# In-projection of a hybrid decoder trunk: the norm's scale moved from the products to the operand, convolution taps from PSUM

## The chip, the cores and the metric

The kernel runs on one core of one Trainium2 chip. The metric is the device time of one execution in microseconds; the kernel before takes 3083.93 us (median of three runs, 3083.13 to 3099.12).

## What is computed

A decoder of two layers on 1040 tokens (16 learned tokens and 1024 of the sequence) with 1024 channels:

```python
for layer in range(DEPTH):                                  # 2
    hn = rmsnorm(h, norm_mix_w[layer])                      # h * rsqrt(mean(h*h) + eps) * w
    proj = hn @ w_in[layer]                                 # 1024 x 3336
    hq, hf, hi, hg, gq, gk, gv, gz, ga, gb, su = split(proj)
    y_a = hgrn2_mixer(hq, hf, hi, hg, ...)
    y_b = gdn_mixer(gq, gk, gv, gz, ga, gb, conv_w, ...)    # qkv = silu(causal_conv4(concat(gq, gk, gv)))
    y_c = s5_mixer(su, ...)
    h = h + concat(y_a, y_b, y_c) @ w_out[layer]
    h = h + square(relu(rmsnorm(h, norm_mlp_w[layer]) @ mlp_w1[layer])) @ mlp_w2[layer]
return rmsnorm(h, final_norm_w)[:, N_META:]
```

The convolution is causal, per channel, with four taps: token t needs the products of t-3 to t.

## The kernel before

Channels lie on the partitions and tokens along the free axis, so `h` is eight tiles of 128 channels (`KD`). The tokens are worked in two blocks of 520 (`T`); a block (l, b) is layer l, tokens b. The dense products are made in halves: an operand x is split into a high part (`xh`) and the rest (`xl`), weights likewise (`wh`, `wl`), and a product of 128 columns is, for each of eight k, the three pairs xh wh, xl wh, xh wl on two runs of 260 tokens (`HN`): 48 matmuls into one PSUM tile `pd` of two banks. Two `pd` tiles exist. A weight granule of four k is loaded by DMA, its high part made by ScalarE (`wh`, L458) and its low part by GpSimd, POOL in the profile (`wl`).

Before a block, `normed` makes xh and xl of h times the norm's weight, tile by tile, as the tiles of h are finished; the norm's scale, one number per token, is not in them. `square` adds up the squares of h, `scale` turns their sum (a matmul with ones on all partitions) into the tile `r` with Ln and Exp. Each product is then multiplied by `r` when VectorE takes it out of PSUM (`scaled`). The two S5 products come first and are taken out before `r` is known (`late`), and are multiplied by it afterwards.

`block` then runs the in-projection and the mixers: two S5 products, the eight gate columns (`in_rows`: decay and beta of the gated DeltaNet, worked on 4 to 8 partitions, stored as `rowd`), twelve convolution products (`in_conv`), four z gates, and for each pair of HGRN2 heads q, f, i and a gate. `in_conv` writes the scaled product into a scratch tile `raw` behind three tokens that the block before left in `hist`, keeps its own last three there, makes the first tap on ScalarE and the other three on VectorE from SBUF:

```python
nc.vector.tensor_copy(raw[:, 0:3], self.hist[:, i, :])
self.scaled(raw[:, 3:T + 3], ps)
nc.vector.tensor_copy(self.hist[:, i, :], raw[:, T:T + 3])
self.act(cv, raw[:, 3:T + 3], AF.Copy, scale=w(3))
for t in range(3):
    self.stt(cv, raw[:, t:t + T], w(t), cv, ALU.mult, ALU.add)
```

A clamp, the sigmoid (three ScalarE passes), a multiplication on POOL and a store follow. Scratch tiles of 520 tokens have the tag `s`; there are six. In the names of the trace `s<-pd,r` is a scaling out of PSUM, `s<-s,cvw` a tap, `mh`, `nh` and `mt` are scratch of the mixers, `mx` their PSUM.

A scheduler sets the order on each engine: it takes the traced instructions with their priorities (weights are called 1000 instructions ahead) and a model of their times, and writes one fixed order per engine. The engines run it in order and wait on semaphores. Layer 0's blocks are both projected at the start; while the state recurrences of block (0, 0) run, block (0, 1) is projected. Layer 1's blocks each follow an output projection and MLP: those of (0, 0), then block (1, 0), those of (0, 1), then block (1, 1). The mixers of a block run beside the next dense work.

## Time and profile before

| | before |
|---|---|
| median of three runs | 3083.93 us |
| lowest, highest | 3083.13, 3099.12 us |
| span of the profiled execution | 3076.0 us |
| TensorE matmul busy | 92% of the span |
| VectorE, ScalarE, POOL busy | 55%, 42%, 52% |
| mean granted TensorE clock | 0.958 |

The profiled execution's own time is not listed apart from the runs; its span lies 7.9 us under their median, the part of a run outside the first and the last instruction. The clock is the share of full speed that was granted to TensorE. It has two levels, 1.2 and 2.4 GHz, so 0.9 over a stretch means the lower level in a fifth of it. Matmuls of one engine overlap; their busy time in a stretch of pure dense work is all of it.

### The profile page before, as it was taken

How to read it: one execution, taken by the hardware profiler on the slowest of the kernel's cores; microseconds unless marked ns; L12 is line 12 of the kernel's file. 1: busy time of each engine (PE TensorE's matmuls, PEld its weight loads, DVE VectorE, ACT ScalarE, POOL GpSimd, SP SyncE). 2: the span in 40 equal slices, each digit the busy share in tenths (PEclk: the TensorE clock that was granted, in tenths of full speed). 3: DMA queues.
4: the chain of work that ended last, by engine and by line, in shares of the span. 5: the costliest groups of instructions: out<-in, count | busy, mean ns of one | idle time of the engine just before them, and what ended most of it. 6: DMA issues, size and time to landing. Idle time of an engine off the chain costs nothing.

```text
span 3076.0 us, 60588 instructions
## 1 busy us (share of the span) xinstructions
PE 2841.1 (92%) x23513; PEld 2652.0 (86%) x23513; DVE 1703.3 (55%) x3079; ACT 1292.1 (42%) x2621; POOL 1598.3 (52%) x1377
## 2 busy tenths in 40 slices
PE   7777899879999998888999999888999999999998
PEld 7677789879999997878989999887777788999998
DVE  7899976686532248897553224887544322522224
ACT  5534465434443344434443334444544333433332
POOL 3564757465644446746364444677464444444442
PEclk8898899889999999899999999889999999999999
DMA  5646455644433354555443335455443333533332
GB/s 150 189 116 189 138 142 160 167 92 136 126 91 102 93 152 125 153 134 147 131 121 99 91 92 152 124 152 135 136 120 106 98 93 97 160 93 92 91 93 80
DMA packets 641613, 381.20 MB, mean 124 GB/s; under 512 B 166239, under 2 KB 599237, under 8 KB 641325
## 3 DMA queue, kind: packets, MB, share of 16 engines
q1 hardware_dynamic: 641325, 377.31, 44.0%
q8 instruction: 186, 3.05, 0.4%
q14 instruction: 102, 0.84, 0.1%
HBM read 308.52 MB, written 70.43 MB: 123 GB/s over the span
## 4 chain that ended last, share of the span: by engine, by line
PE 58%; DVE 13%; DMA 4%; issue 3%; ACT 2%; POOL 1%; SPq 0%; DVEq 0%; POOLq 0%; ACTq 0%
PE pd L124 49%; PE mxt L124 6%; DVE mh L112 4%; DVE s L115 2%; PE mxh L124 2%; DVE s L112 1%; ACT s L109 1%; DVE s L120 1%; DVE nh L112 1%; DMA wr<-in_w_in_dram 1%; DMA nh<-rowd 1%; DVE xl L115 0%; DMA D<-D 0%; DMA hdr<-h 0%; DVE h L112 0%
## 5 line engine op out<-in xcount | busy, mean ns | idle before, releaser
L112 POOL TENSOR_TENSOR wl<-wr,wh 128x512 fp32r<-128x512 f32 x776 | 1056.1, 1363 | 1128.1 <-ACT wh L458 1021.2
L124 PE MATMUL pd<-xh,wh 128*128 128x260 f32 (+2 forms) x3688 | 833.0, 300 | 50.3 <-DVE s L112 31.5
L124 PE MATMUL pd<-xl,wh 128*128 128x260 f32 (+2 forms) x3688 | 833.1, 299 | 10.9 <-DVE xl L115 8.6
L124 PE MATMUL pd<-xh,wl 128*128 128x260 f32 (+1 forms) x3624 | 817.1, 300 | 18.8 <-POOL wl L112 18.3
L458 ACT CAST wh<-wr 128x512 fp32r<-128x512 f32 x776 | 476.8, 617 | 834.3 <-PE pd L124 731.4
L124 PEld LDWEIGHTS pd<-xh,wh 128*128 128x128 f32 (+1 forms) x3688 | 596.0, 194 | 71.5 <-issue 33.7
L124 PEld LDWEIGHTS pd<-xh,wl 128*128 128x128 f32 x3624 | 588.9, 194 | 37.1 <-POOL wl L112 22.7
L124 PEld LDWEIGHTS pd<-xl,wh 128*128 128x128 f32 (+1 forms) x3688 | 596.6, 193 | 27.5 <-DVE xl L115 9.6
L124 PE MATMUL pd<-uh,wh 128*128 128x260 f32 (+1 forms) x2008 | 470.4, 303 | 10.3 <-DVE h L112 4.6
L124 PE MATMUL pd<-ul,wh 128*128 128x260 f32 (+1 forms) x2008 | 470.8, 302 | 0.0
L124 PE MATMUL pd<-uh,wl 128*128 128x260 f32 (+1 forms) x2008 | 469.2, 302 | 0.3 <-POOL wl L112 0.3
L112 DVE TENSOR_TENSOR h<-h,pd 128x520 f32<-128x520 f32 (+2 forms) x296 | 200.1, 677 | 389.0 <-PE pd L124 386.5
L109 ACT ACTIVATE s<-s 128x520 f32<-128x520 f32 (+3 forms) x431 | 272.2, 635 | 256.5 <-DVE s L120 169.1
L124 PEld LDWEIGHTS pd<-uh,wh 128*128 128x128 f32 x2008 | 322.5, 190 | 25.9 <-issue 5.4
L124 PEld LDWEIGHTS pd<-uh,wl 128*128 128x128 f32 x2008 | 322.7, 189 | 13.8 <-POOL wl L112 0.7
L124 PEld LDWEIGHTS pd<-ul,wh 128*128 128x128 f32 x2008 | 322.9, 190 | 12.9 <-issue 0.2
L115 DVE SCALAR_TENSOR_TENSOR s<-pd,r 128x520 f32<-128x520 f32 (+2 forms) x137 | 94.1, 691 | 327.4 <-PE pd L124 327.1
L112 DVE TENSOR_TENSOR ul<-s,uh 128x520 fp32r<-128x520 f32 (+1 forms) x129 | 96.2, 747 | 142.3 <-ACT uh L458 142.2
L115 DVE SCALAR_TENSOR_TENSOR s<-s,cvw 128x520 f32<-128x520 f32 x144 | 152.2, 1060 | 16.3 <-ACT s L109 15.4
L112 POOL TENSOR_TENSOR s<-s 128x520 f32<-128x520 f32 x80 | 114.5, 1431 | 51.5 <-ACT s L109 45.0
L112 POOL TENSOR_TENSOR mh<-mh,qh 128x260 f32<-128x260 f32 (+5 forms) x128 | 98.6, 794 | 25.5 <-ACT mh L109 22.1
L112 DVE TENSOR_TENSOR s<-s 128x520 f32<-128x520 f32 (+3 forms) x119 | 98.8, 835 | 15.5 <-ACT s L109 13.6
(250 smaller groups left out, 3302.0 us busy)
## 6 DMA issues: line engine op xcount, KB each, us to landing
wr<-in_mlp_w_dram SPq DMA_DIRECT2D x512, 256.0 KB
wr<-in_w_in_dram SPq DMA_DIRECT2D x208, 256.0 KB
wr<-in_w_out_dram SPq DMA_DIRECT2D x64, 256.0 KB
qkvd<-s SPq DMA_DIRECT2D x48, 260.0 KB
win<-qkvd SPq DMA_DIRECT2D x40, 312.0 KB
hdr<-h SPq DMA_DIRECT2D x32, 260.0 KB
mh<-qkvd SPq DMA_DIRECT2D x40, 208.0 KB
hd<-s SPq DMA_DIRECT2D x32, 260.0 KB
```

Of the source, the lines that this page charges most:

```text
L109: return self.nc.scalar.activation(out, in_, func, **kw)
L112: return (eng or self.nc.vector).tensor_tensor(out, a, b, op)
L115: return self.nc.vector.scalar_tensor_tensor(out, a, s, b, op0, op1)
L120: return e.tensor_scalar(out, a, s1, None, op0)
L124: return self.nc.tensor.matmul(out, lhsT, rhs, start=start, stop=stop, **kw)
L458: self.nc.scalar.copy(hi, src)
```

## The change

In the in-projection alone, `normed_rows` takes the place of `normed`: all eight squares first, then `scale`, then for each tile of h one VectorE pass that multiplies by weight and scale into an `s` tile, and the split of that. The operand is four tokens longer (`HIST`): in front of the block's tokens stand the last four normed tokens of the block before (zeros in the first), put there and kept by POOL. `in_conv` asks for 264 instead of 260 tokens of each run, so that every run contains the products of the tokens before it, and takes all four taps straight from PSUM. Nothing multiplies by the scale after a product any more: the gates clamp out of PSUM, HGRN2's f takes its negative part on VectorE and its positive part on ScalarE, its i is copied by ScalarE, the S5 products are turned to chunks on the way out of PSUM, one half by each of the two engines. `gdn_begin` copies the three groups of gate rows that are needed instead of all. The MLP's norm and products are as before.

```diff
+    def normed_rows(self, h, wcol, b):
+        nc = self.nc
+        xs = [], []
+        acc = self.s()
+        for k in range(KD):
+            self.square(acc, h[k], k)
+        self.squares, self.r = acc, None
+        r = self.scale()
+        if b == 0:
+            self.hist = self.tl(self.big, [128, KD, HIST], "hist", 1)
+        for k in range(KD):
+            w = self.prm[:, wcol + k:wcol + k + 1]
+            xn = self.tl(self.sp, [128, T + 8], "s", N_S)[:, :T + HIST]
+            if b == 0:
+                nc.gpsimd.memset(xn[:, :HIST], 0.0)
+            else:
+                nc.gpsimd.tensor_copy(xn[:, :HIST], self.hist[:, k])
+            self.stt(xn[:, HIST:], h[k], w, r, ALU.mult, ALU.mult)
+            if b == 0:
+                nc.gpsimd.tensor_copy(self.hist[:, k], xn[:, T:])
+            hi, lo = self.operand("xh"), self.operand("xl")
+            nc.scalar.copy(hi, xn)
+            self.tt(lo, xn, hi.bitcast(F32), ALU.subtract)
+            xs[0].append(hi)
+            xs[1].append(lo)
+        return xs
...
     def in_conv(self, l, b, xs, i):
-        ps = self.cols(l, C_GQ + 128 * i, xs)
-        raw = self.tl(self.sp, [128, T + 8], "s", N_S)
-        nc.vector.tensor_copy(raw[:, 0:3], self.hist[:, i, :])
-        self.scaled(raw[:, 3:T + 3], ps)
-        nc.vector.tensor_copy(self.hist[:, i, :], raw[:, T:T + 3])
-        cv = self.s()
+        ps = self.cols(l, C_GQ + 128 * i, xs, {c: slice(c * HN, (c + 1) * HN + HIST) for c in range(2)})
+        cv, sg = self.s(), self.s()
         w = lambda t: self.cvw[:, l * 48 + t * 12 + i:l * 48 + t * 12 + i + 1]
-        self.act(cv, raw[:, 3:T + 3], AF.Copy, scale=w(3))
+        at = lambda t: ps[:, :, HIST - 3 + t:HIST - 3 + t + HN]
+        self.act(self.half(cv), at(3), AF.Copy, scale=w(3))
         for t in range(3):
-            self.stt(cv, raw[:, t:t + T], w(t), cv, ALU.mult, ALU.add)
+            self.stt(self.half(cv), at(t), w(t), self.half(cv), ALU.mult, ALU.add)
         self.ts(cv, cv, NEG, ALU.max)
...
+    def in_silu(self, l, xs, col):
+        t, n = self.s(), self.s()
+        self.ts(self.half(n), self.cols(l, col, xs)[:, :, :HN], NEG, ALU.max)
+        self.silu(n, t)
+        return t
...
     def in_s5(self, l, xs):
-        products = [lambda t=t: self.cols(l, C_SU + 128 * t, xs) for t in range(2)]
-        return [self.spill(u, "ud", 4) for u in self.late(products, True)]
+        n = (NC + 1) // 2 * CH
+        us = []
+        for t in range(2):
+            ps = self.cols(l, C_SU + 128 * t, xs, {0: slice(HIST, HIST + n), 1: slice(HIST + n, HIST + T)})
+            u = self.s()
+            for c, copy in ((0, self.nc.vector.tensor_copy), (1, self.nc.scalar.copy)):
...
     def in_hgrn(self, l, xs, j):
-        r = self.half(self.scale())
-        self.stt(self.half(mn), ps, 0.0, r, ALU.min, ALU.mult)
-        self.stt(self.half(mx), ps, 0.0, r, ALU.max, ALU.mult)
+        self.ts(self.half(mn), ps, 0.0, ALU.min)
+        self.act(self.half(mx), ps, AF.Relu)
...
-        self.scaled(vt, ps)
+        self.nc.scalar.copy(self.half(vt), self.cols(l, C_HI + 128 * j, xs)[:, :, :HN])
...
     def block(self, l, b, h, hook=None, first=False):
-        xs = self.normed(h, 8 * l)
+        xs = self.normed_rows(h, 8 * l, b)
```

The scheduler writes a new order for the whole program. Three places of it follow; in them `xN` behind a row means that it stands N times in a row, and line numbers of the change are one higher.

VectorE, the norm of block (1, 0), behind the MLP of block (0, 0). Before (`h<-h,pd` adds a product of the MLP to h, `s<-s` adds a square, `ul<-ys,uh` belongs to the next output projection):

```order
L112 TENSOR_TENSOR h<-h,pd 128x520
L112 TENSOR_TENSOR ul<-ys,uh 128x520
L115 SCALAR_TENSOR_TENSOR xl<-h,prm,xh 128x520
L112 TENSOR_TENSOR s<-s 128x520
L112 TENSOR_TENSOR h<-h,pd 128x520
L112 TENSOR_TENSOR ul<-ys,uh 128x520 x2
L115 SCALAR_TENSOR_TENSOR xl<-h,prm,xh 128x520
L112 TENSOR_TENSOR s<-s 128x520
L112 TENSOR_TENSOR ul<-ys,uh 128x520
L538 COPY s<-pd 128x520 x2
L112 TENSOR_TENSOR s<-s,r 128x65x8 x2
```

The change, from the last addition to h:

```order
L113 TENSOR_TENSOR h<-h,pd 128x520
L113 TENSOR_TENSOR ul<-ys,uh 128x520
L113 TENSOR_TENSOR s<-s 128x520
L113 TENSOR_TENSOR ul<-ys,uh 128x520
L116 SCALAR_TENSOR_TENSOR s<-h,prm,r 128x520 x6
L113 TENSOR_TENSOR xl<-s,xh 128x524 x5
L116 SCALAR_TENSOR_TENSOR s<-h,prm,r 128x520
L113 TENSOR_TENSOR xl<-s,xh 128x524
L116 SCALAR_TENSOR_TENSOR s<-h,prm,r 128x520
L113 TENSOR_TENSOR xl<-s,xh 128x524 x2
L676 COPY s<-pd 128x33x8 x2
```

Before, seven of the eight operand tiles stand between the additions to h, and one behind the last; now sixteen operations stand between the last addition and the first eviction.

TensorE at the same place. Before, the sum of squares (`pd<-s,ones`) stands behind the S5 products:

```order
L124 MATMUL pd<-xh,wh 128x260 x2
L124 MATMUL pd<-xl,wh 128x260 x2
L124 MATMUL pd<-xh,wl 128x260 x2
L124 MATMUL pd<-s,ones 128x260 x2
L124 MATMUL pd<-xh,wh 40x260
```

The change (`uh,wl` ends the MLP's last product):

```order
L125 MATMUL pd<-uh,wl 128x260 x2
L125 MATMUL pd<-s,ones 128x260 x2
L125 MATMUL pd<-xh,wh 128x264
L125 MATMUL pd<-xh,wh 128x256
L125 MATMUL pd<-xh,wh 128x264
L125 MATMUL pd<-xh,wh 128x256
L125 MATMUL pd<-xl,wh 128x264
```

Between the MLP's last product and the first S5 product nothing else stands on TensorE.

POOL at the same place in the change (before, the row of `wl` simply goes on):

```order
L113 TENSOR_TENSOR wl<-wr,wh 128x512 x76
L518 MEMSET s 128x4 x6
L523 COPY hist<-s 128x4 x6
L518 MEMSET s 128x4 x2
L523 COPY hist<-s 128x4 x2
L113 TENSOR_TENSOR wl<-wr,wh 128x512
```

The sixteen pieces of four tokens stand in one row, and the next granule's low part behind them.

## Rows read from the trace of the kernel before

**Rows 1.** The page's part 1: busy time of each engine, share of the span, instructions.

```profile
PE 2841.1 (92%) x23513; PEld 2652.0 (86%) x23513; DVE 1703.3 (55%) x3079; ACT 1292.1 (42%) x2621; POOL 1598.3 (52%) x1377
```

**Rows 2.** Busy time by stretch; columns: stretch, its length, engines, PEclk, DMA share, GB/s.

```profile
20.00:282.00 262.00, 204.09 (x1467) 193.90 (x1466) 230.82 (x486) 121.14 (x245) 136.35 (x100) 0.87 0.55 148
282.00:400.00 118.00, 96.22 (x1059) 88.83 (x1059) 104.50 (x188) 56.17 (x123) 76.85 (x70) 0.90 0.60 169
400.00:590.00 190.00, 177.69 (x1677) 162.72 (x1675) 119.94 (x232) 100.58 (x239) 112.92 (x110) 0.94 0.53 148
1165.00:1363.00 198.00, 160.84 (x1221) 156.55 (x1219) 182.29 (x342) 88.46 (x182) 124.45 (x92) 0.91 0.53 137
1937.00:2129.00 192.00, 153.20 (x1166) 148.40 (x1165) 164.44 (x244) 88.31 (x183) 133.58 (x102) 0.89 0.54 142
1700.00:1800.00 100.00, 100.00 (x837) 100.00 (x836) 24.55 (x36) 32.83 (x53) 44.83 (x35) 1.00 0.31 91
```

**Rows 3.** The chain of waits, by line, in the stretch 1165 to 1363.

```profile
by line: DVE s L115 18.8%; DVE mh L112 16.8%; issue 11.1%; DVE s L112 6.7%; DVE s L120 6.0%; ACT s L109 5.7%; DVE nh L112 5.3%; DVE RT L112 3.2%; DVE s L620 2.6%; DVE s L629 2.2%; DMA diag<-MAd 2.2%; DVE xl L112 2.0%; DMA rowd<-s 1.9%; DVE 
```

**Rows 4.** Timeline of VectorE: first and last of twelve convolution evictions (start, length, what).

```profile
1165.11 0.70 DVE L112 TENSOR_TENSOR s<-pd,r 128x520 f32<-128x520 f32 x1
...
1261.73 0.69 DVE L112 TENSOR_TENSOR s<-pd,r 128x520 f32<-128x520 f32 x1
```

**Rows 5.** Groups by line and shape, VectorE: count, busy us, mean ns, idle before.

```profile
L115 DVE SCALAR_TENSOR_TENSOR s<-s,cvw 128x520 f32<-128x520 f32 x144 | 152.2, 1060 | 16.3 <-ACT s L109 15.4
L115 DVE SCALAR_TENSOR_TENSOR s<-pd,r 128x520 f32<-128x520 f32 x105 | 72.6, 696 | 251.6 <-PE pd L124 251.3
L120 DVE TENSOR_SCALAR s<-s 128x520 f32<-128x520 f32 x84 | 66.5, 792 | 1.0
L112 DVE TENSOR_TENSOR s<-pd,r 128x520 f32<-128x520 f32 x88 | 60.7, 689 | 27.8 <-PE pd L124 25.5 <-DMA hd<-s 2.1
L115 DVE SCALAR_TENSOR_TENSOR xl<-h,prm,xh 128x520 fp32r<-128x520 f32 x56 | 51.8, 932 | 15.9 <-ACT xh L109 15.9
L631 DVE COPY hist<-s 128x3 f32<-128x3 f32 x48 | 24.0, 499 | 0.8
L629 DVE COPY s<-hist 128x3 f32<-128x3 f32 x48 | 21.7, 453 | 2.4 <-POOL s L112 1.5 <-DMA qkvd<-s 0.8
L112 DVE TENSOR_TENSOR s<-s,r 128x520 f32<-128x520 f32 x14 | 19.6, 1459 | 21.6 <-ACT r L109 21.6
```

**Rows 6.** The tile of the taps' weights: min/median/max ns; idle before, and until what.

```profile
L115 DVE SCALAR_TENSOR_TENSOR s<-s,cvw x144: 721/758/4155, 67.1 to 2034.2; 128x520 f32<-128x520 f32 x144
  DMA rowd<-s: 21.4, 4
```

**Rows 7.** Timeline, the norm of block (1, 0): last addition to h up to the scale.

```profile
1140.33 0.68 DVE L112 TENSOR_TENSOR h<-h,pd 128x520 f32<-128x520 f32 x1
...
1141.68 0.62 ACT L109 ACTIVATE s<-h 128x520 f32<-128x520 f32 x1
...
1143.93 0.69 DVE L112 TENSOR_TENSOR s<-s 128x520 f32<-128x520 f32 x1
1147.99 0.69 DVE L538 COPY s<-pd 128x520 f32<-128x520 f32 x1
...
1151.78 1.04 PE L124 MATMUL pd<-s,ones 128*128 128x260 f32 x4
...
1154.36 0.60 ACT L109 ACTIVATE r<-pd 128x520 f32<-128x520 f32 x1
1154.98 0.64 ACT L109 ACTIVATE r<-r 128x520 f32<-128x520 f32 x1
```

**Rows 8.** Groups, POOL: the weights' low parts, and the smallest copy.

```profile
L112 POOL TENSOR_TENSOR wl<-wr,wh 128x512 fp32r<-128x512 f32 x776 | 1056.1, 1363 | 1128.1 <-ACT wh L458 1021.2 <-PE pd L124 27.2 <-DMA mh<-in_s_lam_im_dram 18.4
...
L1186 POOL COPY SC<-CB 8x80 f32<-8x80 f32 x8 | 3.2, 396 | 4.2 <-DVE CB L1179 3.8
```

**Rows 9.** Busy time and granted clock just after TensorE had waited.

```profile
1190.00:1192.00 2.00, 2.00 (x12) 2.00 (x11) 2.00 (x3) 2.00 (x5) 1.79 (x2) 0.50 0.80 250
```

More of the change, by code (lines that the diff above doesn't have):

```diff
@@ L44 @@
 TINY = 1e-19
+HIST = 4
 GELU_C = 2.0 * math.sqrt(2.0 / math.pi)
@@ L469, in granule_now @@
         if keep:
-            lo, hi = [self.tl(self.big, [128, T], tag, 8, F32R)[:, :512].rearrange("p (k m) -> p k m", k=4) for tag in ("xl", "xh")]
+            lo, hi = [self.operand(tag)[:, :512].rearrange("p (k m) -> p k m", k=4) for tag in ("xl", "xh")]
         else:
@@ L482, in product, with columns @@
     def product(self, wts, xs, runs=None):
+        ps = self.columns(wts, xs, {c: self.run_of(c) for c in runs or self.runs})
+        return ps[:, :len(self.runs), :self.nh]
+    def columns(self, wts, xs, runs):
         xh, xl = xs
@@ L488, in product, with operand @@
             for i, (w, x) in enumerate(((wh, xh), (wh, xl), (wl, xh))):
-                for c in runs or self.runs:
-                    self.mm(ps[:, c, :self.nh], w[:, k % 4, :], x[k][:, self.run_of(c)],
+                for c, cs in runs.items():
+                    self.mm(ps[:, c, :cs.stop - cs.start], w[:, k % 4, :], x[k][:, cs],
                             start=(k == 0 and i == 0), stop=(k == kn - 1 and i == 2))
-        return ps[:, :len(self.runs), :self.nh]
+        return ps
+    def operand(self, tag):
+        return self.tl(self.big, [128, T + HIST], tag, 8, F32R)
+    def normed_rows(self, h, wcol, b):
[24 more added lines that the diff above has]
+        return xs
     def normed(self, h, wcol):
@@ L499, in normed @@
             w = self.prm[:, wcol + k:wcol + k + 1]
[L500 to L501 removed]
+            hi, lo = self.operand("xh")[:, :self.nt], self.operand("xl")[:, :self.nt]
             self.act(hi, h[k], AF.Copy, scale=w)
@@ L526, in scale, with late @@
         return self.r
-    def scaled(self, out, ps):
-        self.tt(self.half(out), ps, self.half(self.scale()[:out.shape[0]]), ALU.mult)
-    def late(self, products, chunks):
+    def late(self, products):
         ts = []
@@ L536, in late, with cols @@
             t = self.s()
-            if chunks:
-                self.nc.vector.tensor_copy(self.half(t), product())
-            else:
-                self.act(self.half(t), product(), AF.Relu)
+            self.act(self.half(t), product(), AF.Relu)
             ts.append(t)
-        if not chunks:
-            for t in ts:
-                self.tt(t, t, self.scale(), ALU.mult)
-            return ts
-        os = [self.s() for _ in ts]
-        for o, t in zip(os, ts):
-            c = lambda a: a.rearrange("p (c j) -> p c j", j=CH)
-            self.tt(o.rearrange("p (j c) -> p c j", j=CH), c(t), c(self.scale()), ALU.mult)
-        return os
+        for t in ts:
+            self.tt(t, t, self.scale(), ALU.mult)
+        return ts
     def silu(self, n, out):
-        self.ts(n, n, NEG, ALU.max)
         self.sigma(out, n)
         self.tt(out, out, n, ALU.mult, eng=self.nc.gpsimd)
-    def cols(self, l, col, xs):
-        return self.product(self.ready.pop((l, col), None) or self.in_weights(l, col), xs)
+    def cols(self, l, col, xs, runs=None):
+        wts = self.ready.pop((l, col), None) or self.in_weights(l, col)
+        return self.columns(wts, xs, runs or {c: slice(HIST + c * HN, HIST + (c + 1) * HN) for c in range(2)})
     def in_weights(self, l, col):
@@ L591, in in_rows @@
         self.tt(xv, xv, ps[32:40, :, :HN], ALU.add)
-        self.tt(x[0:8], x[0:8], self.scale()[0:8], ALU.mult)
         self.ts(u[0:8], x[0:8], NEG, ALU.max)
@@ L1261, in out_mlp @@
             nc.sync.dma_start(t, self.YS[b][k][:, T - self.nt:])
-            for half_, (tag, bufs) in zip(xs, (("uh", NY), ("ul", NY)) if k < NY else (("xh", 8), ("xl", 8))):
-                half_.append(self.tl(self.big, [128, T], tag, bufs, F32R)[:, :self.nt])
+            for half_, tag in zip(xs, ("uh", "ul") if k < NY else ("xh", "xl")):
+                half_.append((self.tl(self.big, [128, T], tag, NY, F32R) if k < NY else self.operand(tag))[:, :self.nt])
             self.split(t, xs[0][k], xs[1][k])
@@ L1316, in halves @@
             return step
-        for t in self.late([lambda j=j: hidden(0, j) for j in range(2)], False):
+        for t in self.late([lambda j=j: hidden(0, j) for j in range(2)]):
             second_operand(0, t)
```

43 lines of the change are left out of this document (17 added, 26 removed).

## Prediction

> **What bounds the kernel now.** I read the page's busy times first, then the same by stretch, then the chain of waits in one stretch, and the groups last. Over the whole span TensorE is busy 92% and VectorE 55% [rows 1], which looks like a TensorE kernel; that is an average over two kinds of stretch. In the MLPs (1700 to 1800) TensorE is busy all the time at full clock, 837 matmuls in 100 us or 0.12 us each, so a product of 48 takes 5.7 us, and VectorE is busy a quarter [rows 2]. In the in-projections it is the other way round: VectorE is busy 88% from 20 to 282 (block (0, 0)), 89% from 282 to 400 (first part of (0, 1)), 92% from 1165 to 1363 (block (1, 0)) and 86% from 1937 to 2129 (block (1, 1)), while TensorE waits and its granted clock falls to 0.87 to 0.91 [rows 2]. Only the second part of (0, 1), 400 to 590, belongs to TensorE (94%). In (1, 0) twelve convolution products are evicted between 1165.11 and 1261.73 [rows 4], 8.8 us apart, where TensorE would need 5.7. The chain of waits there names VectorE: its nine lines that the row shows sum to 64%, the taps (line L115) first with 18.8% [rows 3].
>
> So VectorE time taken out of these four stretches can become time, and work on any engine elsewhere can't.
>
> **What it relieves.** All prices are means of groups, for one block of 520 tokens.
> - A convolution loses the scaling out of PSUM (0.689) and two copies of three columns (0.499 and 0.453), and its three taps change their source [rows 5]. A tap from SBUF takes 1.060 on average though the median is 0.758 and the worst 4.155 [rows 5, 6]; the same operation with one operand in PSUM takes 0.696 [rows 5]. The new tap isn't in the trace; I bound it by 0.69 and 1.06 and take 0.696, its nearest row in operation, shape and source. 0.689 + 0.952 + 3 x 0.364 = 2.73 us, twelve times 32.8.
> - Eight gates (six, and q twice) lose a pass: 0.689 + 0.792 becomes one clamp out of PSUM at 0.69 [rows 5]. 8 x 0.79 = 6.3.
> - HGRN2's f: two passes of 0.696 become one [rows 5], the other goes to ScalarE; twice, 1.4. Its i goes to ScalarE whole: 2 x 0.689 = 1.4.
> - S5: a copy of 0.69 [rows 7] and a turning multiplication of 1.459 [rows 5] become half a turned copy. Between half of the one and half of the other, 0.35 and 0.73, I take 0.5: 2 x 1.65 = 3.3.
>
> Together 45.2 us a block. ScalarE gets the moved reads (one out of PSUM took 0.60 [rows 7]); it is busy 45% in these stretches [rows 2], so I price them at nothing; without that cover they would be about 4 us a block. POOL gets 8 to 16 pieces of four columns, at most 0.40 each [rows 8], and is busy 63% of (1, 0) [rows 2]; nothing as well, unless something waits for them (below). TensorE gets four columns more in 2304 matmuls: at 0.12 us for 260 columns 1.8 ns each, 4 us in all.
>
> **What it adds: the norm.** The operand took one VectorE pass of 0.932 a tile and now takes two [rows 5]: 8 x 0.93 = 7.5 us more (5.5 at the 0.69 of an unhindered pass [rows 7]). In layer 0 this comes off the relief, 45.2 - 7.5 = 37.7. In layer 1 the old pass lay under the MLP, and the new ones stand in front of the projection, where TensorE waits.
>
> That wait is the price of the change. In (1, 0) the last addition to h begins at 1140.33 and the first S5 product is evicted at 1147.99, 7.7 us later, without a gap on TensorE. Now the path is addition 0.68, square 0.62, sum 0.69, matmuls with ones 1.04, Ln 0.60, Exp 0.64 [rows 7], some 4.8 us with six hand-offs of under 0.1; then sixteen VectorE passes at 0.69 to 0.93, 11.0 to 14.9 us, since the order puts all of them in front of the first eviction; then the last tile's matmuls, 0.7. That is 16.5 to 20.4 instead of 7.7. The matmuls with ones no longer stand behind the S5 products, which gives 1.0 back: 8 to 12 us. The order has nothing for TensorE to do in between. After such a pause the clock is at the lower level for a while, 0.50 from 1190 to 1192 [rows 9]; 10 us with that. In (0, 0) VectorE's part is counted already, so only the path to the scale is left: 5 us. In (0, 1) the scale can be made beside the recurrences of (0, 0): 2 us.
>
> **The sum.** How much of the relief becomes time I take from the two rows on (1, 0): 0.64 by the chain, 0.92 by the busy share; 0.8. TensorE leaves room for it: a mean clock of 0.91 over 198 us costs 18 of its 161 busy us, so it needs 143, and VectorE would need 182 - 42 = 140.
> - (0, 0): 0.8 x 37.7 - 5 = -25.
> - (0, 1): half of the relief, 22.6 - 7.5 = 15.1, lies in the first part, x 0.8 = 12; of the other half, where TensorE is the bound, I take a quarter, 6; less 2: -16.
> - (1, 0) and (1, 1): the relief without S5, which lies ahead of the stretch, 41.9 x 0.8 - 10 = -23.5 each.
>
> With 4 us of columns that is -84 us. Against the profiled span of 3076.0 it makes 2992; the median of the runs, 3083.93, lies 7.9 above that span, so **3000 us**. With 0.64, no quarter and the dearer waits (13, 13, 8, 3) it is 3038, with 0.92, half of the rest of (0, 1) and the cheaper ones (8, 8, 3, 0) 2966.
>
> **One rule against it.** The taps of one product now read PSUM three times, and the trace says that this is cheaper, 0.696 against 1.060 [rows 5]. The Trainium skill, page "VectorE: DVE Perf Modes", section "Rules for kernel authors", says otherwise: either accept the basic rate from PSUM, or copy to SBUF first if many operations follow. By that rule the taps bring nothing; it is the fourth rival below.
>
> **The rivals.**
> 1. *The projection is paced by scratch, not by VectorE: no change.* Six `s` tiles serve everything; ScalarE sat idle 21.4 us in front of four first taps until the store of the gate rows had freed one [rows 6]. A convolution now holds its PSUM tile until scratch is there and all four taps are done, with two such tiles. If only 0.3 of the relief arrives (41 of 136.6) and the waits cost 27 and the columns 4, it is 3074. Against it: VectorE at 92%. 0.13.
> 2. *The norm becomes a barrier: slower.* POOL's pieces stand between VectorE's passes (scratch, zeros, multiplication, copy), and the low parts of the next weights behind them. With 16 pieces of 0.40 in the path (6.4), three low parts of 1.36 behind it [rows 8] (4.1), all passes at 0.93 (14.9), one product at half clock (5.7 more) and the 5.5 of path and last tile, less 7.7, a block loses 29 us, four 116; relief at 0.64 is 87: with the columns 3116. It decides from 22 us a block. Against it: VectorE needs POOL's piece only for the split, and six can be made ahead. 0.10.
> 3. *All of it.* The relief arrives in full and (0, 1) gives its second half too, 159 us, less 27 and 4; and half of what the lower clock costs in three stretches, 18, 21 and 34 us [rows 2], comes back: 2920. For it: with VectorE at 70% TensorE pauses less. Against it: other waits of 11% stand in the chain as issue [rows 3]. 0.12.
> 4. *Taps from PSUM cost 1.06 too.* Then 13.1 us a block go, 38 of the sum: 3038. Against it: 105 passes of this form at 0.696, beside a busy POOL. 0.05.
>
> **Chances.** Forecast 0.60, the rivals as given. About 0.5%, 15 us, can be told from no change. Faster: 0.60 + 0.12 + 0.05 = 0.77; same 0.13; slower 0.10. The range runs from 2930 to 3085: it holds forecast, first and fourth rival and about half of the third, 0.84, and leaves out the barrier.
>
> **What the profile after would show.** Right: taps at 0.70 with a narrow spread; convolution evictions of (1, 0) under 7.5 us apart; VectorE near 80% in the projections and TensorE's clock there above 0.93; a gap of about 10 us on TensorE ahead of both blocks of layer 1, none in the MLPs; the dense part of the MLPs unchanged. Wrong: a first eviction more than 30 us behind the last addition to h, POOL or scratch as what VectorE waits for there; evictions still 8 to 9 us apart with VectorE no longer full, which would be scratch or PSUM; taps over 0.9.

## The result, and the profile after

The changed kernel takes 3057.3 us (median of 4 runs, 3048.9 to 3058.0) where the kernel before took 3088.8 beside it (4 runs, 3083.1 to 3099.1): ratio 0.9893, 95% interval 0.9878 to 0.9908, or 33 us less by that ratio (the medians lie 31.5 apart). The sign was forecast; the size was 84. The spans of the two profiled executions differ by 20.6 us (3076.0 and 3055.4), less than the medians, so sums of profile rows below are made against 20.6 and ratios against 33.

The page's part 1 after, against [rows 1]:

```profile
PE 2826.1 (92%) x23513; PEld 2637.9 (86%) x23513; DVE 1562.6 (51%) x2905; ACT 1298.7 (43%) x2657; POOL 1580.1 (52%) x1425
```

VectorE lost 140.7 us of busy time; four blocks at 45.2 - 7.5 were forecast to lose 150.8. The relief arrived. TensorE's idle time did not follow: span less busy time is 234.9 us before and 229.3 after.

Busy time by stretch after (columns as in [rows 2]): the projections of (0, 0) and (0, 1) in three pieces, then for (1, 0) and again for (1, 1) the norm up to the first convolution eviction, the convolutions, and the z and HGRN2 products behind them.

```profile
20.00:281.00 261.00, 195.32 (x1466) 185.02 (x1466) 204.50 (x453) 115.09 (x249) 135.14 (x117) 0.89 0.59 156
281.00:400.00 119.00, 91.98 (x961) 83.07 (x962) 86.77 (x167) 59.20 (x128) 62.42 (x68) 0.83 0.52 138
400.00:587.00 187.00, 184.46 (x1819) 173.56 (x1819) 102.84 (x215) 108.42 (x260) 119.88 (x120) 1.00 0.63 169
1131.00:1165.40 34.40, 26.65 (x194) 25.70 (x195) 17.13 (x27) 17.20 (x31) 17.91 (x26) 0.85 0.62 171
1165.40:1255.50 90.10, 82.56 (x663) 81.26 (x662) 64.90 (x109) 49.82 (x119) 60.33 (x53) 0.96 0.59 159
1255.50:1349.10 93.60, 75.19 (x566) 72.37 (x564) 77.50 (x206) 38.62 (x69) 52.18 (x38) 0.91 0.58 139
1922.40:2011.10 88.70, 81.54 (x665) 80.28 (x664) 64.19 (x108) 49.79 (x119) 60.35 (x53) 0.98 0.60 161
2011.10:2104.00 92.90, 75.37 (x572) 71.32 (x570) 68.74 (x94) 41.15 (x76) 65.76 (x51) 0.94 0.54 128
```

The same cuts of the kernel before, which [rows 2] show as one stretch for each block:

```profile
1165.10:1270.50 105.40, 85.35 (x662) 83.44 (x661) 97.20 (x144) 51.20 (x116) 70.72 (x54) 0.90 0.51 134
1270.50:1362.40 91.90, 75.13 (x560) 73.02 (x558) 84.41 (x197) 37.16 (x67) 53.73 (x39) 0.91 0.56 142
1930.80:2037.50 106.70, 85.81 (x653) 83.94 (x653) 96.24 (x144) 51.44 (x116) 70.79 (x54) 0.87 0.50 132
2037.50:2127.90 90.40, 72.49 (x565) 69.75 (x564) 72.03 (x103) 39.27 (x72) 64.42 (x50) 0.92 0.56 146
```

| stage (profiled executions, us) | before | after | moved | forecast |
|---|---|---|---|---|
| start to the last addition to h before (1, 0) | 1140.3 | 1131.3 | -9.1 | -41 |
| (1, 0): norm, to the first convolution eviction | 24.8 | 34.1 | +9.3 | +10 |
| (1, 0): convolutions | 105.4 | 90.1 | -15.3 | -26 |
| (1, 0): z and HGRN2 | 91.9 | 93.6 | +1.7 | -7 |
| from there to the last addition before (1, 1) | 542.7 | 537.8 | -4.9 | 0 |
| (1, 1): norm | 25.7 | 35.5 | +9.8 | +10 |
| (1, 1): convolutions | 106.7 | 88.7 | -18.0 | -26 |
| (1, 1): z and HGRN2 | 90.4 | 92.9 | +2.5 | -7 |
| rest | 948.1 | 951.4 | +3.3 | 0 |

The forecast column is that of the prediction, its 0.8 put on 32.8 us of convolutions and 9.1 us behind them. The norm is right to a microsecond. The convolutions give little more than half of it. Behind them nothing arrives. In layer 0 TensorE idled 92 us from 20 to 590 before [rows 2] and idles 95 from 20 to 587 now: 66, 27 and 3 in the three pieces, where it was 58, 22 and 12.

Groups on VectorE after (count, busy, mean ns, idle before), and the line of the taps' weights by tile (min/median/max ns):

```profile
L116 DVE SCALAR_TENSOR_TENSOR s<-pd,cvw,s 128x520 f32<-128x520 f32 x144 | 108.6, 754 | 46.4 <-ACT s L110 41.6 <-POOL s L113 2.8
L121 DVE TENSOR_SCALAR s<-pd 128x520 f32<-128x520 f32 x40 | 27.6, 689 | 25.7 <-PE pd L125 25.7
L116 DVE SCALAR_TENSOR_TENSOR s<-h,prm,r 128x520 f32<-128x520 f32 x32 | 23.6, 780 | 5.0 <-ACT r L110 5.0
L113 DVE TENSOR_TENSOR xl<-s,xh 128x524 fp32r<-128x524 f32 x32 | 21.0, 692 | 1.1 <-ACT xh L525 0.9
```

```profile
L116 DVE SCALAR_TENSOR_TENSOR s<-pd,cvw,s x144: 721/759/761, 64.0 to 2008.4; 128x520 f32<-128x520 f32 x144
```

A tap out of PSUM takes 754 ns and never more than 761, where the taps from SBUF had a median of 758 but reached 4155 [rows 6]. What the change saved on a tap is its tail, and VectorE now stands idle 41.6 us in front of taps, waiting for ScalarE's first one.

Timeline of the norm of (1, 0) after, against [rows 7]: last addition to h, matmuls with ones, the operand's passes, the first S5 eviction.

```profile
1131.25 0.68 DVE L113 TENSOR_TENSOR h<-h,pd 128x520 f32<-128x520 f32 x1
...
1133.86 1.19 PE L125 MATMUL pd<-s,ones 128*128 128x260 f32 x4 [3.26 <-DVE s L113]
...
1136.39 4.11 DVE L116 SCALAR_TENSOR_TENSOR s<-h,prm,r 128x520 f32<-128x520 f32 x6 [2.06 <-ACT r L110]
1137.21 7.69 POOL L523 COPY hist<-s 128x4 f32<-128x4 f32 x6 [2.00 <-DVE s L116]
...
1140.42 3.15 DVE L113 TENSOR_TENSOR xl<-s,xh 128x524 fp32r<-128x524 f32 x5
...
1144.97 1.28 ACT L525 CAST xh<-s 128x524 fp32r<-128x524 f32 x2 [3.75 <-POOL s L518]
...
1150.01 0.65 DVE L676 COPY s<-pd 128x264 f32<-128x264 f32 x1 [3.02 <-PE pd L125]
```

18.8 us from the addition to the eviction; 16.5 to 20.4 were forecast. Six of POOL's copies of four columns take 7.7 us, and the seventh tile waits 3.75 for them. The fifth of the six alone runs from 1139.90 to 1143.63, about as long as VectorE's five passes beside it (1140.42 to 1143.57). VectorE goes through its sixteen passes almost without a pause (1136.39 to 1146.99), so that wait lies beside the path and not in it.

### The profile page after: what moved, and what is told of

The parts are those of the page before. It is cut to its first block, busy times and chain, and to the rows that moved or that the text cites. A ratio compares the mean times of both kernels' runs of the same rounds, so it can differ in the third digit from the quotient of the medians.

```text
span 3055.4 us, 60525 instructions
## 1 busy us (share of the span) xinstructions
PE 2826.1 (92%) x23513; PEld 2637.9 (86%) x23513; DVE 1562.6 (51%) x2905; ACT 1298.7 (43%) x2657; POOL 1580.1 (52%) x1425
## 3 DMA queue, kind: packets, MB, share of 16 engines
q1 hardware_dynamic: 641325, 377.31, 45.2%
## 4 chain that ended last, share of the span: by engine, by line
PE 45%; DVE 5%; issue 1%; DMA 1%; POOL 1%; ACT 1%; SPq 0%; DVEq 0%; POOLq 0%; ACTq 0%
PE pd L125 39%; PE mxt L125 4%; PE mxh L125 1%; DVE mh L113 1%; DVE s L116 1%; POOL wl L113 0%; DVE s L113 0%; ACT s L110 0%; DMA wr<-in_w_in_dram 0%; DVE s L121 0%; DMA nh<-rowd 0%; DVE mt L113 0%; POOL mh L113 0%; DVE ul L113 0%; DVE s L642 0%
## 5 line engine op out<-in xcount | busy, mean ns | idle before, releaser
L113 POOL TENSOR_TENSOR wl<-wr,wh 128x512 fp32r<-128x512 f32 x776 | 1025.2, 1323 | 1079.5 <-ACT wh L459 1012.3
L125 PE MATMUL pd<-xh,wh 128*128 128x260 f32 (+4 forms) x3688 | 832.3, 299 | 59.2 <-DVE s L116 21.2
L125 PE MATMUL pd<-xl,wh 128*128 128x260 f32 (+3 forms) x3688 | 830.1, 298 | 17.8 <-DVE xl L113 10.4
L125 PE MATMUL pd<-xh,wl 128*128 128x260 f32 (+2 forms) x3624 | 814.1, 299 | 11.0 <-POOL wl L113 10.7
L125 PEld LDWEIGHTS pd<-ul,wh 128*128 128x128 f32 x2008 | 321.4, 189 | 12.8
L116 DVE SCALAR_TENSOR_TENSOR s<-pd,r 128x520 f32<-128x520 f32 (+2 forms) x121 | 83.6, 692 | 330.8 <-PE pd L125 330.5
L116 DVE SCALAR_TENSOR_TENSOR s<-pd,cvw,s 128x520 f32<-128x520 f32 x144 | 108.6, 754 | 46.4 <-ACT s L110 41.6
L113 DVE TENSOR_TENSOR s<-s 128x520 f32<-128x520 f32 (+3 forms) x119 | 106.0, 895 | 21.8 <-ACT s L110 20.5
```

The source lines that it names most:

```text
L113: return (eng or self.nc.vector).tensor_tensor(out, a, b, op)
L116: return self.nc.vector.scalar_tensor_tensor(out, a, s, b, op0, op1)
L125: return self.nc.tensor.matmul(out, lhsT, rhs, start=start, stop=stop, **kw)
```

## The experiments

Two theories. LIMITS: VectorE time is worth much less than 0.8, since other limits stand close behind it. NORM: the relief arrives at 0.8 and the norm eats it. All ratios are to the kernel before, timed on the same chip beside each run; 0.001 is 3 us. "After" stands for the changed kernel, 0.9893.

### What time on VectorE and on TensorE is worth

The same two edits in both kernels: one tap on VectorE instead of three, and 32 matmuls instead of 48 in each convolution product.

```diff
-        for t in range(3):
+        for t in range(1):
             self.stt(cv, raw[:, t:t + T], w(t), cv, ALU.mult, ALU.add)
```

```diff
-            for i, (w, x) in enumerate(((wh, xh), (wh, xl), (wl, xh))):
+            for i, (w, x) in [p for p in enumerate(((wh, xh), (wh, xl), (wl, xh))) if not (self.few and p[0] == 1)]:
```

Before, one tap:

> The kernel before with one of the three VectorE taps of each convolution instead of three (taps 2 and 3 are left out, so the convolution has two taps of four): 96 passes of 1.060 us less, 102 us of VectorE time, all of it in the convolution part of the four in-projections, and nothing else changed. Theory LIMITS (VectorE time freed there is worth about a third, because TensorE and other waits stand right behind it): 25 to 45 us faster than before, ratio 0.985 to 0.992. Theory NORM (the relief arrives at 0.8 as I forecast, and the new norm ate it in the change): about 80 us faster, ratio 0.974 or less.

After, one tap:

> The changed kernel with one of the three taps out of PSUM per convolution: 96 passes of 0.754 us less, 72 us of VectorE time. Theory LIMITS: the convolutions are now paced by TensorE and the second part of the projection is untouched, so 5 to 20 us less than the changed kernel's 3057, ratio to before 0.983 to 0.988. Theory NORM: VectorE still paces them, 0.8 x 72 = 58 us, about 3000, ratio 0.971.

After, 32 matmuls:

> The changed kernel with the middle pair (low part of the operand by high part of the weights) left out of the twelve convolution products of each block: 16 of 48 matmuls less, 768 in all, 92 us of TensorE time at 0.12 us each. Theory LIMITS: TensorE paces the convolution part now (82.5 of 90 us busy), so 40 to 70 us less than the changed kernel's 3057, ratio to before 0.967 to 0.977. Theory NORM (VectorE still paces): under 20 us, ratio above 0.983.

Before, 32 matmuls:

> The kernel before with the same 768 matmuls left out. Both theories hold that VectorE paces the convolutions of the kernel before in the main: 10 to 35 us less, ratio 0.989 to 0.997, most of it in block (0, 1), whose second half belongs to TensorE. If it gains 50 us or more, VectorE did not pace these parts even before, and my reading of 88 to 92% busy was wrong.

| | less VectorE time | less TensorE time (92 us) |
|---|---|---|
| before | 102 us: 0.9856 (0.9840 to 0.9873), -44 us | 0.9979 (0.9966 to 0.9992), -6 us |
| after | 72 us: 0.9917 (0.9902 to 0.9932), no gain on 0.9893 | 0.9775 (0.9760 to 0.9791), -36 us on 0.9893 |

Before, a microsecond of VectorE is worth 44/102 = 0.43 and one of TensorE 0.07. After, one of the taps on VectorE is worth nothing and one of TensorE 0.4. (102 and 72 us are the passes left out times their mean; VectorE's busy time in the profiles falls by 94.2 and 55.0, which makes 0.47 of the 0.43.) None of the four came out as NORM alone would have it, but the range of LIMITS held for the first alone: one tap after was to give 5 to 20 us and gave none, and both runs with 32 matmuls came out just above their ranges (0.9775 for at most 0.977, 0.9979 for at most 0.997). Over the whole kernel the change moved the limit of this work from VectorE towards TensorE. By stretch, the convolutions and what is behind them in (1, 0), for the kernel before with one tap:

```profile
1145.90:1238.40 92.50, 82.53 (x678) 80.78 (x678) 72.03 (x125) 54.62 (x120) 66.47 (x55) 0.96 0.58 157
1238.40:1339.00 100.60, 74.73 (x538) 71.54 (x536) 89.14 (x218) 36.16 (x63) 54.21 (x37) 0.92 0.52 129
```

the convolutions of the changed kernel with one tap:

```profile
1164.50:1252.70 88.20, 81.22 (x653) 80.58 (x652) 55.08 (x91) 52.23 (x124) 61.35 (x56) 0.96 0.61 164
```

and those of the changed kernel with 32 matmuls:

```profile
1136.00:1216.50 80.50, 60.99 (x443) 59.71 (x444) 65.85 (x97) 46.55 (x108) 55.71 (x47) 0.87 0.59 154
```

In the first, 12.9 us come off the convolutions (105.4 before) and 8.7 come back behind them (91.9). In the second VectorE is down to 55 of 88 us and the stretch is 2 us shorter than with three taps: TensorE is busy 81 us of it, 92%. Less work for TensorE does shorten it, by 9.6 us.

A stretch alone doesn't tell what bounds it, though. The kernel before with 32 matmuls, convolutions of (1, 0) and what is behind them:

```profile
1167.90:1255.50 87.60, 61.55 (x424) 60.17 (x424) 84.18 (x121) 46.86 (x96) 60.53 (x44) 0.82 0.50 134
1255.50:1358.10 102.60, 79.52 (x600) 77.97 (x599) 87.95 (x165) 41.35 (x84) 61.17 (x45) 0.90 0.60 150
```

Here the convolutions lose 17.8 us, more than with one tap, and 10.7 come back behind them; the order puts 121 instructions of VectorE into them where 144 stood. Over both parts of both blocks of layer 1, one tap is worth 8.8 us before and 32 matmuls 6.6, so there the two are alike. The difference lies in layer 0, where the last addition to h comes 19.5 us earlier with one tap and 2.6 later with 32 matmuls. After the change, too, 30 of the 46 us by which 32 matmuls shorten the profiled span lie ahead of that addition, 28.5 of them in the convolutions of (0, 1) (115.3 to 86.8), where TensorE had been busy for 109. Each edit also gets an order of its own from the scheduler, and no run holds the order fixed: what that alone does to a stretch is not known.

### The price of the norm

The first try took the scale out of the operand (it multiplies by a one) but still made it:

```diff
-        r = self.scale()
+        r = self.K["ones"][:, 0:1].to_broadcast([128, T])
```

with squares and scale traced behind the operand.

> The changed kernel with the scale left out of the operand (the VectorE pass multiplies h by the norm's weight and by a one; the sum of squares and the scale are still made, behind the operand, and nothing uses them): same instructions, but the operand no longer waits for the last tile of h and the scale. Its time against the changed kernel's 3057 is the price of the barrier. Theory LIMITS (barrier as I sized it, some 10 us in each block of layer 1 and 5 and 2 in layer 0): 20 to 35 us less, ratio to before 0.977 to 0.983. Theory NORM (the barrier ate the forecast gain): 50 us less or more, ratio under 0.973.

0.9927 (0.9906 to 0.9948), no gain, and outside both ranges. The matmul with ones still stood ahead of the S5 products on TensorE, which waits 10.4 us in front of it in both blocks of layer 1: from the last addition to the first convolution eviction it still takes some 31 us. So the next one leaves squares and scale out:

> The changed kernel without squares, sum and scale for the in-projection (the operand pass multiplies by the norm's weight and a one), so that TensorE meets no matmul with ones ahead of the S5 products. The earlier run without the barrier still had that matmul there, and kept 31 us between the last addition to h and the first convolution eviction in both blocks of layer 1 (33 to 35 in the changed kernel, 24 to 25 before). Theory LIMITS: that stretch falls to 24 or 25 us, so layer 1 gains 9 us twice, layer 0 10 to 20, 25 to 40 us in all, ratio to before 0.976 to 0.982. If the norm is not what it costs, the stretch falls but the time stays within 10 us of the changed kernel, ratio 0.987 or more.

0.9782 (0.9767 to 0.9796): 34 us less than after. Timeline of (1, 0) in it, the last addition on VectorE and the first convolution read on ScalarE:

```profile
1111.82 0.68 DVE L113 TENSOR_TENSOR h<-h,pd 128x520 f32<-128x520 f32 x1
```

```profile
1135.10 0.67 ACT L110 ACTIVATE s<-pd,cvw 128x520 f32<-128x520 f32 x1
```

23.3 us instead of 34.1, so 10.8 us in (1, 0); in (1, 1) 12.8; and the addition itself comes 19.4 us earlier, the price in layer 0 (some of the 43 is given back later by the ratio). I had sized waits and the passes of layer 0 at 27 + 0.8 x 15 = 39. NORM, which needed 50 or more, fell. This run also leaves out the squares and their sums, which the kernel before made as well (28 passes of VectorE, 8.8 us of its busy time), so 34 is more likely too much than too little for what the change added.

Three edits to shorten this path in the full computation: the scale of (0, 1) made early (v1); the kept tokens stored as split halves, so that no scratch tile waits for POOL, with the two S5 products interleaved over k (v2); v1 and v2 together (v3); v1, the split halves, and every second low part of the operand on POOL in three blocks (v4).

```diff
             trace(hook)
+            self.early = self.rows_scale(self.nxt[1])
```

```diff
-            nc.scalar.copy(hi, xn)
+            nc.scalar.copy(hi[:, HIST:], xn)
...
+                if b == 0:
+                    nc.gpsimd.memset(x[:, :HIST].bitcast(F32), 0.0)
+                    nc.gpsimd.tensor_copy(keep[:, k], x[:, T:])
+                else:
+                    nc.gpsimd.tensor_copy(x[:, :HIST], keep[:, k])
```

```diff
-            self.tt(lo[:, HIST:], xn, hi[:, HIST:].bitcast(F32), ALU.subtract)
+            self.tt(lo[:, HIST:], xn, hi[:, HIST:].bitcast(F32), ALU.subtract, eng=nc.gpsimd if k % 2 and (l, b) != (0, 1) else None)
```

> The changed kernel, but the squares and the scale of block (0, 1) are made as soon as its h is loaded, during the projection of block (0, 0). In the changed kernel the scale of (0, 1) is finished at 300 us and its first S5 product is evicted at 339, with TensorE at a granted clock of 0.74 from 260 to 340. Theory LIMITS: the operand passes of (0, 1) start about 20 us earlier and up to 15 us of that becomes time, ratio to before 0.984 to 0.990. If those 40 us belong to the recurrences of (0, 0), which run in them: no change, 0.989 to 0.990.

> A version of the changed kernel with a shorter path through the norm: the four preceding tokens are kept as split halves and put into the operand by POOL behind the operand's passes, so that no scratch tile waits for POOL, and the two S5 products run interleaved over k, so that TensorE works on both while the operand tiles arrive. Theory LIMITS: the stretch from the last addition to h to the first convolution eviction falls from 33.4 and 34.8 us to 28 or 30 in layer 1, some 5 us each, and a few in layer 0: 8 to 20 us less than the changed kernel, ratio 0.983 to 0.987. If something behind it takes the gain back: 0.988 or more.

> The same with the scale of block (0, 1) made during the projection of (0, 0) as well. That edit alone gave no measurable gain (ratio 0.9896). Both together: between the gain of the shorter norm path alone and 10 us more, ratio 0.980 to 0.987.

> The changed kernel with three edits to the norm's path: the scale of block (0, 1) made early, the four preceding tokens kept as split halves (so that no scratch tile waits for POOL), and in three of the four blocks every second low part of the operand made by POOL instead of VectorE. Theory LIMITS (the operand passes in front of the projection are the price, 11 to 13 us on VectorE): the stretch from the last addition to the first convolution eviction falls from 34 to 30 us in layer 1, ratio to before 0.981 to 0.986. If POOL becomes the longer chain: 34 us or more, 0.987 or more.

v1 0.9896 (0.9870 to 0.9922), v2 0.9892 (0.9877 to 0.9906), v3 0.9866 (0.9849 to 0.9882), v4 0.9874 (0.9858 to 0.9890). None is clear of 0.9893 (0.9878 to 0.9908), and in layer 1 the stretch from the addition to the first convolution eviction stayed at 34 to 36 us in all of them (34.1 and 35.5 after). v1 and v2 came out as said for no gain, v4 as said for POOL as the longer chain, and v3 at the upper end of its range. TensorE has three pauses on this path in layer 1: until the sum of squares, until the first high part of the operand and until its first low part. They are 8.2 us in the change (3.3, 2.9 and 2.0 in (1, 0)), 8.2 in v2 and v3 and 9.2 in v4, and behind them it has no pause over 0.25 us up to the first convolution eviction. The edits shorten none of the three. That the price lies in VectorE's passes alone is not shown.

### What paces the part behind the convolutions

First the triangular solve, its substitutions left out of both kernels.

```diff
-        for i in range(1, H):
+        for i in range(1, 1):
...
-        for dst, a, bt in ((mid, low(Dg), Tm[:, 0:H, 0:H]), (low(Tm), Tm[:, H:, H:], mid)):
+        for dst, a, bt in ():
```

> The changed kernel without the substitutions of the triangular solve of the gated DeltaNet (the inverse is left at the identity): some 24 products and sums per block less on VectorE, over 20 us of it, and some passes on POOL, all behind the twelve convolutions. Theory LIMITS: evictions of the z and HGRN2 products stand behind the solve on VectorE, 10 us apart where TensorE would need 6, so 35 to 70 us less than the changed kernel over four blocks, ratio to before 0.967 to 0.978. If TensorE or the weights pace that part instead: under 15 us, ratio above 0.984.

> The kernel before without the same substitutions. Theory LIMITS: the z and HGRN2 part took the same 92 us before (91.9) as after the change (93.7) in block (1, 0), because the solve paces it in both: about the same gain as the same edit gives in the changed kernel, 35 to 70 us, ratio 0.977 to 0.989. If VectorE was full of evictions there before, and is no longer, the gain is larger before than after by 20 us or more.

After 0.9734 (0.9712 to 0.9757), 49 us on 0.9893; before 0.9768 (0.9743 to 0.9793), 71 us. But of the part in question only (1, 1) became shorter, 92.9 to 82.0 us after and 90.4 to 77.7 before; in (1, 0), where VectorE also builds the S5 tables, it stayed (95.4 after, 90.0 before), and much of the gain lies in layer 0 (the last addition to h comes 40 us earlier after, of 61 in the profiled span, and 31 of 66 before). The gain is 22 us larger before than after; 20 or more was to mean that VectorE had been fuller there before, but each of the two gains is uncertain by some 7 us. The solve is a cost of both kernels; that it paces this part is shown for (1, 1) only.

Then the weights of the z and HGRN2 products: a constant tile instead (neither loaded nor split) after and before, where one column of it is repeated; loads left out but both passes kept; loads issued from ScalarE's queue; and POOL's low part alone left out.

```diff
-        wts = self.ready.pop((l, col), None) or self.in_weights(l, col)
+        kept = C_GZ <= col < C_GA or col < C_GQ
+        wts = [(self.kept, self.kept)] * 2 if kept else self.ready.pop((l, col), None) or self.in_weights(l, col)
```

For the other three, in the granules of these columns, shortened to what differs (the constant as source; the other queue; the high part twice):

```diff
-        raw = self.tl(self.big, [128, 4, 128], "wr", N_W)
+        raw = self.K["ones"].unsqueeze(1).to_broadcast([128, 4, 128])
```

```diff
-self.nc.sync.dma_start(raw, v[g])
+self.nc.scalar.dma_start(raw, v[g])
```

```diff
-        self.split(raw, hi, lo, self.nc.gpsimd)
-        return hi, lo
+        self.nc.scalar.copy(hi, raw)
+        return hi, hi
```

> The changed kernel with one constant weight tile kept on chip for the z and HGRN2 products (their weights are neither loaded nor split: 24 loads, 24 passes of ScalarE and 24 of POOL less per block; the matmuls are the same). The part of the projection behind the convolutions took 93.6 and 92.9 us in layer 1, where TensorE needs 68 at full clock. If late weights pace it, in SP's queue behind stores that wait for VectorE (one such wait of 7.25 us stands at 1317), it falls to 75 to 85 us, 30 to 60 us over four blocks, ratio to before 0.970 to 0.980. If the evictions behind the solve pace it: it stays above 88 us, ratio 0.983 or more.

> The kernel before with one constant weight tile for the z and HGRN2 products (neither loaded nor split), as in the run on the changed kernel, where the part behind the convolutions fell from 93 to 78 and 82 us and the whole to a ratio of 0.975. If supply of weights and VectorE's evictions both stood close behind each other there before the change, as theory LIMITS has it: a smaller gain than the 45 us of the changed kernel, 10 to 35 us, ratio 0.989 to 0.997. If the supply of weights paced this part before as much as after: 45 us, ratio 0.985 or less.

> The changed kernel with the loads of the z and HGRN2 weights left out, but the passes of ScalarE and POOL that split them kept (they read a constant). The matmuls are the same. If the loads in SP's queue are what was late: the part behind the convolutions is 78 to 84 us as without loads and passes, ratio 0.973 to 0.979. If it was ScalarE's and POOL's passes: 90 us and more, ratio 0.986 or more.

> The changed kernel with the loads of the z and HGRN2 weights issued from ScalarE's queue instead of SP's; nothing is left out. If they were late because they stand in SP's queue behind stores that wait for VectorE and POOL: the part behind the convolutions falls by 5 to 12 us a block, ratio to before 0.977 to 0.985. If they are late because their buffers come free late, or because ScalarE now waits for buffers in front of its evictions: no gain, 0.989 or more.

> The changed kernel without POOL's low part of the z and HGRN2 weights alone (the high part stands in for it; loads and ScalarE's casts are as they were, and so are the matmuls). Leaving out loads and both passes took 45 us off, leaving out the loads alone nothing. If it is POOL (the low part comes late behind POOL's other passes, and VectorE's passes over SBUF are slower beside it): the part behind the convolutions falls from 93 to 78 to 84 us with VectorE's busy time in it from 77.5 to under 70, ratio to before 0.974 to 0.981. If it is ScalarE's cast, queued behind sigmoids that wait for VectorE's evictions: 89 us or more, ratio 0.986 or more.

| weights of z and HGRN2 | ratio | this part in (1, 0), (1, 1) |
|---|---|---|
| as they are, after | 0.9893 | 93.6, 92.9 |
| neither loaded nor split, after | 0.9746 (0.9731 to 0.9760) | 77.5, 81.8 |
| neither loaded nor split, before | 0.9881 (0.9858 to 0.9904) | 77.0, 86.4 |
| not loaded, but split | 0.9895 (0.9875 to 0.9914) | 88.6, 93.8 |
| loaded from ScalarE's queue | 0.9900 (0.9881 to 0.9919) | 91.7, 94.3 |
| no low part on POOL | 0.9826 (0.9809 to 0.9844) | 84.7, 89.3 |

Three of these came out as one of their two readings said: the constant tile after, as late supply; the loads left out, as the passes; the other queue, as no gain. Two lie between their readings: the constant tile before (37 us, where 10 to 35 or 45 were said) and the run without low parts (0.9826, where at most 0.981 or at least 0.986 was said).

The loads are not it, although TensorE's longest wait there was for a cast behind a late load. Waits of TensorE in this part of (1, 0) after, 1255 to 1350 (us in total, times, longest):

```profile
PE pd L125 <- ACT wh L459: 7.2, 1, 7.2
PE pd L125 <- DVE s L121: 3.7, 3, 2.9
PE mxh L417 <- DVE nh L121: 2.8, 2, 1.9
PE pd L125 <- DVE xl L113: 2.4, 2, 1.6
PE pd L125 <- POOL wl L113: 2.1, 2, 1.7
```

Without loads that 7.2 was replaced by other waits. POOL's low parts are about half of it (21 of 45 us); the row without them, against 1255.50 to 1349.10 above:

```profile
1245.70:1330.40 84.70, 73.65 (x573) 71.51 (x571) 66.17 (x204) 39.46 (x71) 25.91 (x18) 0.96 0.63 152
```

and with neither loads nor passes:

```profile
1234.60:1312.10 77.50, 70.59 (x566) 69.97 (x564) 66.45 (x211) 26.92 (x47) 22.18 (x15) 0.96 0.39 90
```

With POOL down from 52 to 26 us, VectorE does practically the same work (204 instructions, 206 before) in 66.2 us instead of 77.5, and in (1, 1) in 59.4 instead of 68.7 (99 and 94 instructions). The same limit stood there before the change: 37 us from the same edit against 45 after. The other half goes with ScalarE's casts in one order with sigmoids that wait for VectorE's evictions (35 us of waiting on ScalarE in this part); that was not taken out by itself and stays argued.

Last, v4 with one of the two low parts of each z and HGRN2 weight on VectorE (`onv`: second granule of these columns):

```diff
-        self.split(raw, hi, lo, self.nc.gpsimd)
+        self.split(raw, hi, lo, None if self.onv else self.nc.gpsimd)
```

> The version with the early scale, the split history and the operand's low parts shared with POOL (ratio 0.9874 alone), and one of the two low parts of each z and HGRN2 weight made by VectorE instead of POOL: 12 passes of some 0.7 us more on VectorE per block, 12 of 1.3 less on POOL. If POOL paces that part: 5 to 20 us better than without, ratio 0.981 to 0.986. If VectorE does: no better, 0.987 or more.

0.9874 (0.9858 to 0.9891), the same as v4 and what was said for VectorE as the limit. This part is 87.2 us in (1, 0) and 92.1 in (1, 1), where v4 has 92.2 and 90.4, and VectorE is busy in it for 71.3 and 69.3 where it was 79.6 and 69.0: POOL's relief doesn't come back as VectorE's busy time, and why nothing of it is left over the whole is not shown.

## Why the prediction was right or wrong

- **What bounds, and the parts' prices: right.** Over the whole kernel VectorE's time in the convolutions was worth six times TensorE's before (0.43 and 0.07 a microsecond), though not in layer 1 taken by itself, and its busy time fell by 140.7 of 150.8 us. The taps were mis-sized by little: 754 ns instead of 696, 0.17 us on a convolution's 2.73. POOL's pieces were bounded at 0.40 and took 1.18 (copies out of scratch) and 0.55 on average, 0.66 and 0.19 in the median: a few that ran beside VectorE's row of passes took up to 6.9. One tile in (1, 0) waited 3.75 us for them, beside the path. In the sums one slip: the lower end, 2966, leaves out the 4 us of columns that 3038 counts; with them it is 2970.
- **The norm: right.** 10 a block in layer 1, measured 9.3 and 9.8 in the change and 10.8 and 12.8 with it taken away; at most some 34 us in all by the ratios. The barrier rival decided from 22 us a block and stayed far from it.
- **"How much of the relief becomes time": wrong, and it is the step that made 84 of 33.** I took 0.8 between 0.64 (VectorE's share of the chain) and 0.92 (its busy share). Measured directly it is 0.43 in the kernel before, 0.47 by VectorE's busy time. The change itself agrees: 33 us, and the 34 for the norm, are 67 of 140.7, or 0.48. A share of the chain says how often an engine is the last to arrive, and nothing of how far behind it the next one is.
- **"TensorE leaves room for it": wrong in the same way.** I set 143 us of TensorE against 140 of VectorE for the whole stretch of (1, 0). Split in two, the convolutions hold 663 matmuls, 79 us at the 0.12 of the MLPs [rows 2], and 32.8 of the relief: they went to 90.1, with TensorE busy 82.6. The part behind them needs 68 us of TensorE, had 9.1 of relief, and is held by VectorE, POOL and ScalarE together; it took 92 before and 94 now. So 15 and 18 us came where 26 was forecast, and +2 twice where -7 was.
- **Layer 0: -9 instead of -41.** The norm cost 19 there, as in the sum (7 of waits and 0.8 x 15 of passes); the relief gave 28 where 60 stood, by the same step. In the projection of (0, 0), at 120 to 132 us, TensorE now waits 12.4 us for the loads of the input of (0, 1) where it waited 2.2: part of the waiting on VectorE became waiting on a load. What that costs no run shows.
- **The rivals.** All of it: fell; two more taps taken off VectorE gave nothing, though the solve taken off gave 49 us. Taps at 1.06: fell, 0.754. Scratch: its number, 3074 with 0.3 of the relief, was nearer than mine, but its mechanism is a small part: TensorE waits 5.5 us in 90 for taps that hold PSUM, and VectorE 2.8 us over the whole span for a POOL pass that feeds a tap. A seventh scratch tile was not tried.
- **The rule against the change.** The Trainium skill, "VectorE: DVE Perf Modes", section "Rules for kernel authors", names two ways: accept the basic rate from PSUM, or copy out of PSUM first if many operations follow. The change took the first. Three taps from PSUM at 754 ns replaced a pass and three taps at 1060, so for these passes, beside POOL, the measurement decides against the copy; without POOL beside them the taps from SBUF took 753, the same as those from PSUM.
- **What would show it.** Spread of the taps, pause ahead of layer 1 and its length, full MLPs: as said. The convolutions were to be under 7.5 us apart: 7.7. VectorE near 80%: 72% in the convolutions, 83% and 74% behind them. Clock above 0.93: 0.96 and 0.98 in the convolutions, 0.91 and 0.94 behind.

## What to carry to other kernels

Before turning relief on one engine into time, take the next limit stretch by stretch: for each part of the stage, the busy time at full clock of every other engine, and what each stands in order with. A run that removes a known piece of the suspected engine's work (here two taps) prices it directly, and the same edit after the change tells whether the bound has moved. Such a run is read over the whole and not by one stretch: what came off the convolutions came back behind them in part, whichever engine had been relieved. A long wait in the trace is not yet worth its length: the 7.2 us for a weight vanished with the loads, and the time stayed.

## What the hardware showed

A VectorE pass with one operand in PSUM and one in SBUF keeps its time beside POOL: of the 144 taps after, 118 run beside a pass of POOL, and all take between 721 and 761 ns. Of the 144 with both operands in SBUF [rows 6], the 38 that run beside none take 753 on average and 762 at most, and the 106 others 1170 on average and up to 4155. The longest, in the kernel before, and what POOL did beside it:

```profile
2010.84 4.16 DVE L115 SCALAR_TENSOR_TENSOR s<-s,cvw 128x520 f32<-128x520 f32 x1 [0.50 <-ACT s L109]
2010.89 1.06 POOL L112 TENSOR_TENSOR mh<-nh,tri 104x416 f32<-104x416 f32 x1
2011.92 1.27 POOL L112 TENSOR_TENSOR s<-s 128x520 f32<-128x520 f32 x1
2013.16 1.27 POOL L112 TENSOR_TENSOR wl<-wr,wh 128x512 fp32r<-128x512 f32 x1
```

It ends half a microsecond behind the last of POOL's three. It goes the other way too: in the norm after, POOL's copy of four columns that stands beside VectorE's five passes over two SBUF operands takes 3.73 us, where the shortest take 0.18.

The Trainium skill, "SBUF — State Buffer", section "Who interferes with whom", says so: a VectorE instruction with two SBUF inputs contends with a GpSimd instruction that reads SBUF, one with at most one SBUF input outside the 2-port modes does not. The traces agree in both halves, 1170 against 753 ns and 761 at most. That is what the change gains on a tap. For the passes behind the convolutions their sum agrees (66.2 us of VectorE instead of 77.5 without POOL's low parts), but not every group: of two groups of the solve over two SBUF operands, `mh<-Tm,diag` 80x507 fell from 2358 to 1872 ns in that run and `mh<-nh,Tm` 80x507 rose from 1986 to 2709, and the solve's own passes on POOL stayed. The next thing to try, which was not tried: other VectorE passes over two SBUF operands behind the convolutions, given one operand in PSUM.
